# The first down projection of a decoder trunk: the third block product moved ahead of the seventh, its sums made by adding transfers

## The chip, the cores and the metric

The kernel runs on one core of a Trainium2 chip. The metric is the device time of one execution in microseconds (us); it is given as the median of three runs. The engines are named as in the profile: PE (TensorE, matrix products), PEld (its weight loads), DVE (VectorE), ACT (ScalarE), POOL (GpSimd) and SP (SyncE, which here only issues transfers).

## The reference

The computation is one layer of a decoder for 512 tokens of width 1024, all in float32. The changed place is the product with `w_down` in the first of the two SwiGLU blocks.

```python
def swiglu(x, w_gate, w_up, w_down):
    return (jax.nn.silu(x @ w_gate) * (x @ w_up)) @ w_down
...
        x = x + 0.5 * swiglu(rmsnorm(x, ffn1_norm[l]), ffn1_wg[l], ffn1_wu[l], ffn1_wd[l])
        x = x + hybrid_mixer(rmsnorm(x, mix_norm[l]), w_in[l], conv_w[l], conv_b[l], ...)
        x = x + 0.5 * swiglu(rmsnorm(x, ffn2_norm[l]), ffn2_wg[l], ffn2_wu[l], ffn2_wd[l])
    return rmsnorm(x, final_norm)
```

`w_down` has 2816 rows and 1024 columns. The mixer that follows normalises the new rows of x and multiplies them by `w_in`.

## The kernel before

**Products in three parts.** The matrix products keep nearly float32 accuracy on inputs that are rounded to a shorter type (`fp32r`). A weight tile is split into its rounded part `wh` (a copy on ACT) and the remainder `wl` (a subtraction on DVE); the other operand is split in the same way into `ch` and `cl` (`cx` for a narrower pair). PE then multiplies three times: `wh,ch`, `wh,cl` and `wl,ch`. So every tile needs an ACT and a DVE instruction before PE can use it.

**The down projection in quadrants.** `block_down` cuts the operand and the weight into quadrants and forms the product from seven products of sums and differences of quadrants (instead of eight plain ones). Products 1 and 2 take weight blocks as they come from memory (`wr`). Products 5, 6, 3 and 7 take sums of weight blocks. Four of the weight's blocks per row pair are numbered `blocks(0, n)` to `blocks(3, n)`, n = 0 to 4. The operands are differences of quadrants of the hidden rows, held in tiles named `ha`, `hb` and `cr`. The hidden rows are 2816 = 22 x 128; twenty of these groups go into the ten steps of each product (`pairs` = 10, two quadrants), and a "joined" step per product, written `(p, x)`, takes the remaining ones with weight sums `sj`.

**Steps.** The stage is a list, `steps`, of 78 entries. Before the change the order of products is 1, 2, 5, 6, 7, 3, 4:

- steps 0 and 1: the joined steps of products 1 and 2; 2 to 11: product 1; 12 to 21: product 2
- 22 to 31: product 5; 32 and 33: joined steps of 5 and 6; 34 to 43: product 6
- 44 to 53: product 7; 54 and 55: joined steps of 7 and 3; 56 to 65: product 3
- 66: joined step of 4, 67 empty, 68 to 77: product 4

Each step is six matmuls of 128x512: two row groups `m`, three products each (`products1`). Two steps share one *unit*, a 128x1024 pair `wh`, `wl`.

**What sets the order.** The loop at the end of the quoted code walks over the steps, and the order of the code is the order of each engine's queue (`tc.manual_schedule`). Before step i's turn everything else is placed by a step index: `task(i, ...)` puts work into a table, and `tasks_at(i)` emits it behind the products of step i. The unit of a pair is at its step less 4; its operand at its step less `before`; weight fetches further ahead. `then1(i, ...)` does the same for work outside `block_down`: row loads, squares, turned quadrants, and the first fetches of the mixer. SP is the usual queue for transfers (`Q`), POOL the one (`G`) for adding transfers, which add what they read from memory to a tile.

**PSUM.** Each product accumulates in two banks (one for each row group). `CHAIN` lets products 6, 7 and 4 go on in the bank pair of product 1, and product 3 in that of product 5; product 2 has a pair named `aux`. When a product ends, `results1` issues two DVE instructions `xr<-mm,xr` that add the bank's sums, with factor plus or minus 0.5, to a quadrant of the rows `xr`. The next product in the same banks can't go on until DVE has read them.

```python
    ADDS = {1: [(0, 0, -1)], 5: [(1, 1, 1)], 6: [(1, 0, -1)], 3: [(1, 0, -1)], 7: [(1, 1, 1)], 2: [(0, 0, 1)], 4: [(0, 1, 1)]}
    CHAIN = {6: 1, 7: 1, 4: 1, 3: 5}
```

Around `turn_`, before the last step of product 6 (step 43), the loop interleaves the two row groups of steps 42 and 43 and of 44 and 45, so that the first group's sums are complete a while before product 7 wants their bank.

**The weight sums before.** For products 5 and 6 a tile `sm` per row pair is loaded by SP (`blocks(2, n)`), and POOL adds `blocks(3, n)` and later `blocks(0, n)`. For product 7, SP loads the fourths into half tiles `a` (`blocks(3, n)`, ten half loads `a<-w1d`), and DVE subtracts them from `sm` into a new tile `s` (`less`, two instructions `s<-sm,a` of 128x512 per pair). Then POOL adds `blocks(1, n)` to `sm` for product 3. Product 4 splits its weights straight from the fourths, `a`. The operand of product 7, `ch`/`cl` from `cr`, is split six steps ahead.

The names in the profile that have line L250 are issued by the planner's wrapper (`emit`), and transfers have line L238 (`dma_start`).

Of the kernel before, what the change touches and what calls it, by code (L numbers as in the profile page):

```python
# [9 lines left out]
F32 = mybir.dt.float32  # L10
F32R = mybir.dt.float32r
AF = mybir.ActivationFunctionType
ALU = mybir.AluOpType

P = 128
# [240 lines left out]
def hybrid_kernel(ctx, tc, xt, xrow, vec, w1s, w1u, w1d, wm, wki, wrg, watt, wrnn, wout, w2u, w2d, gf, out):  # L256
# [26 lines left out]
    def nm(s):  # L283
        cnt[0] += 1
        return f"{s}_{cnt[0]}"

    def slot(dt=F32, name="s", last=False):
        if loans and last:
            return loans.pop()
        if mixing:  # L290
            plan.free("slot", SLOTS - 2 * COUPLES)
            held = plan.live["slot"]
            spare = [h for h in mixing if plan.key(h) not in held]
            if spare and dt is F32:
                return plan.take("slot", spare[-last])
        return plan.take("whole", plan.take("slot", big.tile([P, S], dt, tag="slot", name=nm(name))))
# [766 lines left out]
    def block_down(wd, plain, pairs, sums, made=None):  # L1063
# [9 lines left out]
        if made:  # L1073
            steps += run_(3, 6) + run_(7) + [(7, x_), (3, x_)] + run_(3, 6, None)
        else:
            steps += run_(7) + [(7, x_), (3, x_)] + run_(3)
        steps += [(4, x_), None] + run_(4)
        index = {s: i for i, s in enumerate(steps)}
        tasks = {}
# [4 lines left out]
        def blocks(b, n):  # L1084
            return wd[b * (pairs // 2) + n]

        units, turned, ra, raws, s7, fourths = {}, {}, {}, {}, {}, {}

        def fetch(key, i):
            def load():  # L1090
                raws[key] = raw.tile([P, WMAX], F32, tag="raw", name=nm("wr"))
                if type(i) is not int:
                    Q.dma_start(raws[key][:, :i.shape[-1]], i)
                    return
                Q.dma_start(raws[key], wd[i])

            return [("SP", 0.6, load, False)]

# [92 lines left out]
        for i in range(0, len(steps), 2):  # L1191
            st = steps[i]
            p, j = st
            if j == pairs:
                if not made:
                    srcs = [lambda k=k: parts_[k] for k in {1: (0, 1), 5: ("w5", 0), 7: (2, 1), 4: (3,)}[p]]
                    task(i - 4, unit(i, *srcs, n=S))
                    continue
                if p in (5, 7):
                    task(i - 4, unit(i, lambda n=(5, 7).index(p): joined[n]))  # L1200
                    continue
                key, src = ("joined", p), {1: wd[2 * pairs], 4: wd[2 * pairs + 1][:, S:]}[p]
                used.append([i - 4, key, src])
                task(i - 4, unit(i, lambda key=key, c=src.shape[-1]: raws[key][:, :c], n=src.shape[-1]))
                continue
            n = j // 2
            assert steps[i + 1] == (p, j + 1) and j % 2 == 0
            if p in (1, 2) or p == 4 and made:
                key = (p, n)
                used.append([i - 4, key, {1: 0, 2: 1, 4: 3}[p] * (pairs // 2) + n])  # L1210
                srcs = [lambda key=key: raws[key]]
            elif made:
                key = (p, n)
                used.append([i - 4, key, made[p][n]])
                srcs = [lambda key=key: raws[key]]
            elif p == 7:
                srcs = [lambda n=n: s7[n]]
            elif p == 4:
                srcs = [lambda n=n, k=k: fourths[n][k] for k in range(2)]
            else:  # L1220
                srcs = [lambda n=n: sums[n]]
            if p == 1:
                task(j, lambda n=n: difference(n))
            if p == 2:
                task(i, lambda n=n: reduced(n))
            if p == 5 and not made:
                def base(n=n):
                    sums.append(couple(F32, "sm"))
                    Q.dma_start(sums[n], blocks(2, n))

                def add(n=n):
                    G.dma_start(sums[n], blocks(3, n), accum_op=ALU.add)

                at = SUMS_AT[n]
                task(at, [("SP", 0.6, base, False)])
                task(at + 3, [("POOL", 1.2, add, False)])
            if p == 7 and not made:
                def held(n=n):
                    fourths[n] = [slot(F32, "a4") for _ in range(2)]
                    for k, t in enumerate(fourths[n]):  # L1240
                        Q.dma_start(t, blocks(3, n)[:, k * S:(k + 1) * S])

                def less(n=n):
                    s7[n] = raw.tile([P, WMAX], F32, tag="raw", name=nm("s7"))
                    for k, t in enumerate(fourths[n]):
                        c = slice(k * S, (k + 1) * S)
                        V.tensor_sub(s7[n][:, c], sums[n][:, c], t)

                task(i - 13, held)
                task(i - 6, less)  # L1250
            if p == 6 and not made:
                def second(n=n):
                    G.dma_start(sums[n], blocks(0, n), accum_op=ALU.add)

                task(index[5, j] - 3, second)
            if p == 3 and not made:
                def fourth(n=n):
                    G.dma_start(sums[n], blocks(1, n), accum_op=ALU.add)

                task(index[7, j] - 4, fourth)  # L1260
            before = {1: 6, 6: 6, 7: i - index[5, j] - 1 if made else 6, 4: i - (index[7, j] if made else index[3, j] + 6)}.get(p, 5)
            if p == 6:
                task(i - before - 1, lambda n=n: V.tensor_sub(a(n, lo), b(n, hi), a(n, hi)))
            if p == 4:
                task(i - before - 1, lambda n=n: V.tensor_sub(a(n, lo), b(n, lo), a(n, lo)))
            task(i - before, operand(p, n))
            task(i - 4, unit(i, *srcs))
# [288 lines left out]
    def keep(s_, half, i):  # L1556
        keep_part(parts1[s_, half], half, i, (lo, hi)[s_])

    for i, (s_, half) in zip((3, 8, 12, firsts1[3]), ((0, 0), (1, 1), (1, 0), (0, 1))):
        then1(i, load_rows, s_, half)  # L1560
    for p, s_, half, at in ((2, 0, 0, 4), (7, 1, 1, 3), (3, 1, 0, 3)):
        then1(lasts1[p] + at, turn_part, s_, half)
        for m in range(2):
            then1(lasts1[p] + at + m, square_row, 2 * s_ + m, half)
            then1(lasts1[p] + at + (5 if p == 3 else 1 + m), keep, s_, half, m)
    for k in range(NQ):
        then1(lasts1[7] + 6 + k, lambda k=k: half_row(k, lo, x[k][:, lo]))
        then1(lasts1[3] + 1 + k, lambda k=k: half_row(NQ + k, hi, x[NQ + k][:, hi]))
        then1(lasts1[3] + 4 + k, lambda k=k: half_row(k, hi, turned_part(parts1[1, 0], k)))
    then1(index[3, 0], lambda: A.activation(small.tile([P, 4], F32, tag="st", name=nm("root"))[:, :1], epst, AF.Sqrt))  # L1570
    for n in range(RAWS):
        then1(index[3, 3 + 2 * n], mixer_fetch)
    then1(index[3, 8], key_fetch)
    then1(index[4, 3], key_begin)
    then1(last - 1, mixer_begin)
    with tc.manual_schedule(engines=ENGINES):
        assert min(d1.tasks) >= 0
        plan.clear()
        cs = decay()
        turn_ = lasts1[6]  # L1580
        for i in range(last):
            if i in (turn_ - 1, turn_ + 1):
                for m in range(2):
                    for k in range(2):
                        products1(i + k, (m,))
            elif i not in (turn_, turn_ + 2):
                products1(i)
            if i and i - 1 != turn_:
                results1(i - 1)
            if i == turn_:  # L1590
                results1(i)
            d1.tasks_at(i)
            if i > index[6, 0]:
                next(cs, None)
            for f_, args in late1.pop(i, ()):
                f_(*args)
        results1(last - 1)
        assert not late1
        for m in range(2):
            for i in range(last, len(steps)):  # L1600
                products1(i, (m,))
            if m:
                mixer_begin()
            result1(4, m, *ADDS[4][0])
            square_row(m, 1)
            if not m:
                mixer_prepare()
        sd, rs1 = (small.tile([P, NQ], F32, tag=t, name=nm("rs")) for t in ("st", "m8"))
        V.tensor_add(sd, ssr[:, :NQ], ssr[:, NQ:])
        A.activation(sd, sd, AF.Sqrt, scale=1.0 / D, bias=epst)  # L1610
        V.reciprocal(rs1, sd)
        mixer_prepare()
# [972 lines left out]
```

## Time and profile before

| | |
|---|---|
| median of 3 runs | 1044.96 us (1044.94 to 1046.19) |
| profiled execution: time of its own | 1045.18 us |
| its span in the profile | 1043.4 us, so 1.78 us lie around the span |
| mean granted TensorE clock | 0.996 |
| PE busy | 1028.1 us, 99% of the span |
| DVE, ACT, POOL busy | 905.6, 712.5 and 195.0 us |
| DMA | 202.81 MB, mean 194 GB/s |
| the stage: first matmul of step 2, last matmul of the stage | 229.11 us, 343.61 us |

The span is a single execution from its first to its last recorded event. A row of a timeline gives the start, the duration, the engine, the line, the operation, the tiles (out <- in) and the shapes; in brackets stands the idle time ahead of the instruction and what ended it. DVE, ACT and PE overlap consecutive instructions a little, so the distance between starts is shorter than the duration shown. The waits of an engine are listed with their sum, their number and the longest.

### The profile page before, as it was taken

The numbers are of one execution on the slowest core, as the hardware profiler recorded it, in microseconds if no ns is written. First come the engines' busy times: TensorE is split into PE (matmuls) and PEld (weight loads), VectorE is DVE, ScalarE is ACT, GpSimd is POOL, SyncE is SP. The second block draws the span as 40 slices with busy tenths as digits, with TensorE's granted clock in tenths as the row PEclk, the third lists the DMA queues.
The fourth block names the chain that finished last, engine by engine and source line by source line (L and its number), as shares of the span: only waits on it lengthen the run. The fifth ranks groups of instructions, "written<-read, shape, count | busy, mean of one in ns | idle before, by whom it ended". The sixth has DMA issues, their size and how long they took to land.

```text
span 1043.4 us, 15243 instructions
## 1 busy us (share of the span) xinstructions
PE 1028.1 (99%) x5250; PEld 875.8 (84%) x5250; DVE 905.6 (87%) x1543; ACT 712.5 (68%) x1198; POOL 195.0 (19%) x243
## 2 busy tenths in 40 slices
PE   9999999999979999999999999999999999999997
PEld 8898888898758778888888888888998888898886
DVE  7988999987889888999998976777889999889886
ACT  8856766656548659878879664467667666658864
POOL 1613333213110020101001110012422333210000
PEclk9999999999989999999999999999999999999999
DMA  9969999899870363424349997893979999986454
GB/s 356 205 166 221 214 232 227 200 264 245 208 163 17 109 180 103 132 88 126 122 141 248 258 239 212 237 337 54 202 212 229 219 232 220 201 219 220 167 186 162
DMA packets 91181, 202.81 MB, mean 194 GB/s; under 512 B 18400, under 2 KB 25696, under 8 KB 91104
## 3 DMA queue, kind: packets, MB, share of 16 engines
q1 hardware_dynamic: 60608, 142.27, 40.1%
q0 software_dynamic: 30208, 59.26, 33.2%
q8 instruction: 41, 0.67, 0.3%
q10 hardware_dynamic: 288, 0.31, 0.1%
q14 instruction: 36, 0.29, 0.1%
HBM read 181.88 MB, written 25.17 MB: 198 GB/s over the span
## 4 chain that ended last, share of the span: by engine, by line
PE 93%; DVE 3%; DMA 1%; issue 1%; ACT 1%; POOL 0%; DVEq 0%; ACTq 0%; POOLq 0%
PE mm L250 70%; PE aux L250 23%; DVE wl L250 1%; DMA ha<-cr 1%; DMA wr<-w1d 1%; PE aux L1333 0%; ACT wh L250 0%; DVE xr L250 0%; DVE cl L250 0%; DVE s L250 0%; POOL ha L238 0%; DVE cr L250 0%; DVE o L250 0%; DVE kw L250 0%; DVE KI L250 0%
## 5 line engine op out<-in xcount | busy, mean ns | idle before, releaser
L250 DVE TENSOR_TENSOR wl<-wr,wh 128x1024 fp32r<-128x1024 f32 (+3 forms) x149 | 177.1, 1189 | 29.2 <-ACT wh L250 28.7
L250 ACT ACTIVATE wh<-wr 128x1024 fp32r<-128x1024 f32 (+2 forms) x148 | 153.1, 1035 | 37.6 <-PE mm L250 18.8
L250 PE MATMUL mm<-cm,wh 128*128 128x512 f32 (+1 forms) x736 | 167.0, 354 | 0.0
L250 PEld LDWEIGHTS mm<-cm,wh 128*128 128x128 f32 x736 | 126.3, 190 | 15.8
L250 PE MATMUL mm<-yn,wh 128*128 128x512 f32 x420 | 130.7, 392 | 0.0
L250 PE MATMUL aux<-cm,wh 128*128 128x512 f32 (+1 forms) x472 | 119.5, 383 | 0.0
L250 PE MATMUL mm<-cm,wl 128*128 128x256 f32 x608 | 108.3, 282 | 0.0
L250 PE MATMUL mm<-wh,ch 128*128 128x512 f32 (+1 forms) x240 | 94.0, 392 | 7.2 <-DVE xr L250 7.2
L250 PEld LDWEIGHTS aux<-cm,wh 128*128 128x128 f32 x472 | 86.0, 188 | 15.6
L250 PEld LDWEIGHTS mm<-cm,wl 128*128 128x128 f32 x608 | 92.2, 190 | 4.7
L250 PE MATMUL mm<-wl,ch 128*128 128x512 f32 (+1 forms) x240 | 94.0, 392 | 0.1
L250 PE MATMUL mm<-wh,cl 128*128 128x512 f32 (+1 forms) x240 | 93.5, 389 | 0.0
L250 PEld LDWEIGHTS mm<-yn,wh 128*128 128x128 f32 x420 | 77.2, 188 | 14.6
L250 PE MATMUL mm<-yn,wl 128*128 128x512 f32 x210 | 81.9, 390 | 0.0
L250 ACT ACTIVATE wh<-a 128x1024 fp32r<-128x1024 f32 (+1 forms) x78 | 62.8, 814 | 19.7 <-DVE a L250 17.2
L250 DVE TENSOR_TENSOR wl<-a,wh 128x1024 fp32r<-128x1024 f32 (+1 forms) x78 | 71.2, 918 | 5.7 <-ACT wh L250 5.0
L250 PE MATMUL aux<-cm,wl 128*128 128x256 f32 x456 | 70.5, 282 | 0.0
L250 PEld LDWEIGHTS aux<-cm,wl 128*128 128x128 f32 x456 | 63.1, 191 | 1.9
L250 PE MATMUL mm<-yh,wh 128*128 128x512 f32 x160 | 62.7, 394 | 0.0
L250 PE MATMUL mm<-yh,wl 128*128 128x512 f32 x160 | 62.1, 390 | 0.0
L250 PE MATMUL mm<-yl,wh 128*128 128x512 f32 x160 | 62.1, 390 | 0.0
L250 PEld LDWEIGHTS mm<-wh,ch 128*128 128x128 f32 x240 | 45.5, 189 | 16.6 <-ACT wh L250 7.6
(392 smaller groups left out, 2320.0 us busy)
## 6 DMA issues: line engine op xcount, KB each, us to landing
wr<-wm SPq DMA_DIRECT2D x39, 512.0 KB, 3.5
w<-w2d SPq DMA_DIRECT2D x20, 512.0 KB, 7.7
wr<-w SPq DMA_DIRECT2D x20, 512.0 KB, 3.5
wr<-w1u SPq DMA_DIRECT2D x19, 512.0 KB, 6.3
s<-w2u SPq DMA_DIRECT2D x36, 256.0 KB, 4.7
wr<-w2u SPq DMA_DIRECT2D x18, 512.0 KB, 6.1
s<-w2u POOLq DMA_DIRECT2D x36, 256.0 KB, 6.6
s<-w1u SPq DMA_DIRECT2D x32, 256.0 KB, 5.3
```

What stands on the lines that cost most here:

```text
L250: return call(*args, **kw)
```

## The change

The change touches `block_down` (in the form that the first down projection uses, `made` is None) and the loop that runs it.

- The order of products becomes 1, 2, 5, 6, 3, 7, 4. Steps 44 to 53 are now product 3, 54 and 55 the joined steps of 3 and 7, and 56 to 65 product 7.
- The tile `sm` gets `blocks(1, n)` for product 3 by POOL directly behind its use in product 6; no DVE instruction reads it in between.
- Product 7's weights come from new half tiles `s` (slots "s3"): SP loads halves of `blocks(2, n)`, and POOL adds halves of `blocks(0, n)`, two steps behind. That is ten half loads and ten half adding transfers; the ten DVE subtractions and the ten half loads of fourths are gone.
- Product 4's weights are fetched as whole blocks `wr`, five fetches of 512 KB. The first two go out on POOL's queue, the others on SP's.
- The operand of product 7 is split in the fifth product (steps 23 to 31) and no longer six steps ahead of its use.
- Four loads of the rows `xr` go out sooner (steps 2, 6, 9 and the start of product 7).
- The interleaving of row groups is now around the last step of product 7 (step 65), where product 4 goes on in the same banks. The turned quadrants change accordingly: another quadrant is turned after product 3 and another after product 7, and four of the eight half-width `yl`/`yh` pairs are made at full width instead.
- The mixer's first fetches move from product 3 to product 4, four steps ahead of their old places in it.

```diff
-            steps += run_(7) + [(7, x_), (3, x_)] + run_(3)
+            steps += run_(3) + [(3, x_), (7, x_)] + run_(7)
...
-                Q.dma_start(raws[key], wd[i])
+                late = not made and key in ((4, 0), (4, 1))
+                (G if late else Q).dma_start(raws[key], wd[i])
...
-                    srcs = [lambda k=k: parts_[k] for k in {1: (0, 1), 5: ("w5", 0), 7: (2, 1), 4: (3,)}[p]]
+                    srcs = [lambda k=k: parts_[k] for k in {1: (0, 1), 5: ("w5", 0), 3: (1, 2), 4: (3,)}[p]]
...
-            if p in (1, 2) or p == 4 and made:
+            if p in (1, 4, 2):
...
             elif p == 7:
-                srcs = [lambda n=n: s7[n]]
-            elif p == 4:
-                srcs = [lambda n=n, k=k: fourths[n][k] for k in range(2)]
+                srcs = [lambda n=n, k=k: s3[n][k] for k in range(2)]
...
             if p == 7 and not made:
-                def held(n=n):
-                    fourths[n] = [slot(F32, "a4") for _ in range(2)]
-                    for k, t in enumerate(fourths[n]):
-                        Q.dma_start(t, blocks(3, n)[:, k * S:(k + 1) * S])
-
-                def less(n=n):
-                    s7[n] = raw.tile([P, WMAX], F32, tag="raw", name=nm("s7"))
-                    for k, t in enumerate(fourths[n]):
-                        c = slice(k * S, (k + 1) * S)
-                        V.tensor_sub(s7[n][:, c], sums[n][:, c], t)
-
-                task(i - 13, held)
-                task(i - 6, less)
+                def base(n=n, k=0):
+                    s3.setdefault(n, []).append(slot(F32, "s3"))
+                    Q.dma_start(s3[n][k], blocks(2, n)[:, k * S:(k + 1) * S])
+
+                def add(n=n, k=0):
+                    G.dma_start(s3[n][k], blocks(0, n)[:, k * S:(k + 1) * S], accum_op=ALU.add)
+
+                for k in range(2):
+                    task(i + k - 14, lambda base=base, k=k: base(k=k))
+                    task(i + k - 12, lambda add=add, k=k: add(k=k))
...
-                task(index[7, j] - 4, fourth)
-            before = {1: 6, 6: 6, 7: i - index[5, j] - 1 if made else 6, 4: i - (index[7, j] if made else index[3, j] + 6)}.get(p, 5)
+                task(index[6, j] - 3, fourth)
+            before = {1: 6, 6: 6, 7: i - index[5, j] - 1, 4: i - (index[7, j] if made else index[3, j] + 6)}.get(p, 5)
...
-    for i, (s_, half) in zip((3, 8, 12, firsts1[3]), ((0, 0), (1, 1), (1, 0), (0, 1))):
+    for i, (s_, half) in zip((2, 6, 9, firsts1[7]), ((0, 0), (1, 1), (1, 0), (0, 1))):
         then1(i, load_rows, s_, half)
-    for p, s_, half, at in ((2, 0, 0, 4), (7, 1, 1, 3), (3, 1, 0, 3)):
+    for p, s_, half, at in ((2, 0, 0, 4), (3, 1, 0, 4), (7, 1, 1, 3)):
         then1(lasts1[p] + at, turn_part, s_, half)
...
     for n in range(RAWS):
-        then1(index[3, 3 + 2 * n], mixer_fetch)
-    then1(index[3, 8], key_fetch)
+        then1(index[4, 3 + 2 * n] - 4, mixer_fetch)
+    then1(index[7, 8], key_fetch)
...
-        turn_ = lasts1[6]
+        turn_ = lasts1[7]
         for i in range(last):
             if i in (turn_ - 1, turn_ + 1):
                 for m in range(2):
-                    for k in range(2):
+                    for k in (0, 1) if i < turn_ else (0, 2):
                         products1(i + k, (m,))
-            elif i not in (turn_, turn_ + 2):
+            elif i not in (turn_, turn_ + 3):
                 products1(i)
```

DVE's queue at the end of the sixth product before the change. `wl` is a weight remainder, `s` the seventh product's sums, `cl` its operand remainder, `cc` small work of another stage, `xr<-mm` the sixth product's row update:

```order
L250 TENSOR_TENSOR wl_3137<-s_530_3111,wh_3136 128x1024
L250 TENSOR_TENSOR s_537_3140<-sm_2408,a_513_3039 128x512
L250 TENSOR_TENSOR s_537_3140<-sm_2408,a_514_3040 128x512
L250 TENSOR_TENSOR cl_3144<-cr_2643,ch_3143 128x512
L250 SCALAR_TENSOR_TENSOR cc<-cc,zt_3068 128x8 x2
L250 TENSOR_TENSOR wl_3169<-s_537_3140,wh_3168 128x1024
L250 TENSOR_TENSOR s_542_3172<-sm_2481,a_519_3064 128x512
L250 TENSOR_TENSOR s_542_3172<-sm_2481,a_520_3065 128x512
L250 TENSOR_TENSOR cl_3176<-cr_2672,ch_3175 128x512
L250 SCALAR_TENSOR_TENSOR cc<-cc,zt_3068 128x8
L250 SCALAR_TENSOR_TENSOR xr_2664<-mm_2608,xr_2664 128x512
L250 SCALAR_TENSOR_TENSOR xr_2664<-mm_2612,xr_2664 128x512
```

Each step of the seventh product brings two subtractions, a weight remainder and an operand remainder here. The same place after the change, where the work ahead of the row update belongs to the third product:

```order
L250 TENSOR_TENSOR wl_3139<-sm_2399,wh_3138 128x1024
L250 SCALAR_TENSOR_TENSOR cc<-cc,zt_3079 128x8
L250 SCALAR_TENSOR_TENSOR cl_3150<-hb_106,ch_3149 128x512
L250 SCALAR_TENSOR_TENSOR cc<-cc,zt_3079 128x8
L250 TENSOR_TENSOR wl_3161<-sm_2408,wh_3160 128x1024
L250 SCALAR_TENSOR_TENSOR cc<-cc,zt_3079 128x8
L250 SCALAR_TENSOR_TENSOR cl_3174<-hb_108,ch_3173 128x512
L250 SCALAR_TENSOR_TENSOR cc<-cc,zt_3079 128x8
L250 SCALAR_TENSOR_TENSOR xr_2654<-mm_2608,xr_2654 128x512
L250 SCALAR_TENSOR_TENSOR xr_2654<-mm_2612,xr_2654 128x512
```

The subtractions `s<-sm,a` are gone, and the operand remainders are those of the third product.

DVE's queue in the fifth product after the change; the rows `cl<-cr` are the seventh product's operand remainders, which did not stand there before:

```order
L250 TENSOR_TENSOR cl_2909<-ha_109,ch_2908 128x512
L250 TENSOR_TENSOR cl_2914<-cr_2616,ch_2913 128x512
L250 TENSOR_TENSOR wl_2924<-sm_2516,wh_2923 128x1024
L250 TENSOR_TENSOR cl_2934<-ha_111,ch_2933 128x512
L250 TENSOR_TENSOR cl_2939<-cr_2643,ch_2938 128x512
L250 TENSOR_TENSOR wl_2961<-sm_2572,wh_2960 128x1024
L250 TENSOR_TENSOR ha_103<-hb_104,ha_103 128x2x256
L250 TENSOR_TENSOR cl_2976<-cr_2672,ch_2975 128x512
```

Before the change the rows between the `wl` and the `cl<-ha` there were the same without the `cl<-cr`.

DVE's queue after the change at the end of the seventh product. `wl_3434` belongs to the unit of step 66, `wl_3458` to that of step 68, and the row update stands behind both:

```order
L250 TENSOR_TENSOR wl_3413<-s_563_3277,wh_3412 128x512
L250 TENSOR_TENSOR wl_3413<-s_566_3290,wh_3412 128x512
L250 TENSOR_TENSOR wl_3434<-sj_2688,wh_3433 128x512
L250 TENSOR_TENSOR wl_3458<-wr_3401,wh_3457 128x1024
L250 SCALAR_TENSOR_TENSOR xr_2654<-mm_2608,xr_2654 128x512
L250 SCALAR_TENSOR_TENSOR xr_2654<-mm_2612,xr_2654 128x512
L250 TENSOR_TENSOR wl_3480<-wr_3425,wh_3479 128x1024
```

Before the change no product went on in the banks of `mm_2608` and `mm_2612` at this place: the third, in the fifth's banks, ended here.

POOL's queue after the change, at the end of the ten adding half transfers (`s`) of the seventh product's sums; `ha` and `hb` from `wrg` belong to the mixer:

```order
L238 DMA s_559_3252<-w1d 128x512
L238 DMA s_560_3261<-w1d 128x512
L250 MEMSET ha_103 128x128
L238 DMA s_563_3277<-w1d 128x512
L250 AFFINE_SELECT ha_103<-ha_103 128x128
L238 DMA ha_103<-wrg 128x256
L238 DMA s_566_3290<-w1d 128x512
L238 DMA wr_3401<-w1d 128x1024
L238 DMA wr_3425<-w1d 128x1024
L238 DMA hb_104<-wrg 128x256 x2
```

Before the change the rows of `ha_103` and `hb_104` followed one another, directly behind the last adding transfer to a whole tile `sm`; the transfers of `s` and `wr` are new in this queue.

More of the change, by code (lines that the diff above doesn't have):

```diff
@@ L1085, in blocks @@
             return wd[b * (pairs // 2) + n]
-        units, turned, ra, raws, s7, fourths = {}, {}, {}, {}, {}, {}
+        units, turned, ra, raws, s3 = {}, {}, {}, {}, {}
         def fetch(key, i):
@@ L1564, in hybrid_kernel @@
             then1(lasts1[p] + at + m, square_row, 2 * s_ + m, half)
-            then1(lasts1[p] + at + (5 if p == 3 else 1 + m), keep, s_, half, m)
+            then1(lasts1[p] + at + (5 if p == 7 else 1 + m), keep, s_, half, m)
     for k in range(NQ):
-        then1(lasts1[7] + 6 + k, lambda k=k: half_row(k, lo, x[k][:, lo]))
-        then1(lasts1[3] + 1 + k, lambda k=k: half_row(NQ + k, hi, x[NQ + k][:, hi]))
-        then1(lasts1[3] + 4 + k, lambda k=k: half_row(k, hi, turned_part(parts1[1, 0], k)))
+        then1(lasts1[7] + 1 + k, lambda k=k: y.append(norm_tile(k, V_GM, False)))
+        then1(lasts1[7] + 5 + k, lambda k=k: half_row(NQ + k, hi, turned_part(parts1[1, 1], k)))
     then1(index[3, 0], lambda: A.activation(small.tile([P, 4], F32, tag="st", name=nm("root"))[:, :1], epst, AF.Sqrt))
     for n in range(RAWS):
-        then1(index[3, 3 + 2 * n], mixer_fetch)
-    then1(index[3, 8], key_fetch)
+        then1(index[4, 3 + 2 * n] - 4, mixer_fetch)
+    then1(index[7, 8], key_fetch)
     then1(index[4, 3], key_begin)
```

## Prediction

> **What bounds the kernel.** I read the page first, for the engine that is the bound and for the slices where it is not.
>
> ```profile
> span 1043.4 us, 15243 instructions
> PE 1028.1 (99%) x5250; PEld 875.8 (84%) x5250; DVE 905.6 (87%) x1543; ACT 712.5 (68%) x1198; POOL 195.0 (19%) x243
> ...
> PE   9999999999979999999999999999999999999997
> ```
>
> PE is busy 99% of the span, so only what keeps PE from working, or its clock, can cost time. Slice 12 (from 287 us) shows a 7. The waits of PE, sorted, name it:
>
> ```profile
> PE mm L250 <- DVE xr L250: 7.2, 1, 7.2
> PE aux L250 <- DVE kw L250: 1.1, 1, 1.1
> ```
>
> One wait carries nearly everything that PE loses: it wants a PSUM bank that DVE's row update `xr<-mm,xr` hasn't yet read. In PE's timeline:
>
> ```profile
> 229.11 0.39 PE L250 MATMUL mm<-wh,ch 128*128 128x512 f32 x1
> ...
> 256.31 0.39 PE L250 MATMUL mm<-wh,ch 128*128 128x512 f32 x1
> ...
> 288.04 0.40 PE L250 MATMUL mm<-wl,ch 128*128 128x512 f32 x1
> 295.66 0.77 PE L250 MATMUL mm<-wh,ch 128*128 128x512 f32 x1 [7.22 <-DVE xr L250]
> ...
> 298.36 0.47 PE L250 MATMUL mm<-wh,ch 128*128 128x512 f32 x1
> ...
> 313.45 0.39 PE L250 MATMUL mm<-wh,ch 128*128 128x512 f32 x1
> ```
>
> From 229.11 to 256.31 lie steps 2 to 21, 120 matmuls: 27.20 / 120 = 0.2267 us each, 1.36 us a step. The sixth product's last matmul starts at 288.04; the seventh's first is due at 288.27 and starts at 295.66. The next six starts take 2.70 us, about 0.43 each, so PE also runs slowly for a while. Step 56, 72 matmuls after 288.27, starts at 313.45. DVE in the gap, grouped (busy us, mean ns, idle before) and by time:
>
> ```profile
> L250 DVE TENSOR_TENSOR s<-sm,a 128x512 f32<-128x512 f32 x6 | 3.9, 684 | 0.0
> L250 DVE TENSOR_TENSOR wl<-s,wh 128x1024 fp32r<-128x1024 f32 x3 | 3.7, 1222 | 0.6 <-ACT wh L250 0.6
> ```
> ```profile
> 289.31 1.28 DVE L250 TENSOR_TENSOR s<-sm,a 128x512 f32<-128x512 f32 x2
> 290.52 0.69 DVE L250 TENSOR_TENSOR cl<-cr,ch 128x512 fp32r<-128x512 f32 x1
> 291.12 0.36 DVE L250 SCALAR_TENSOR_TENSOR cc<-cc,zt 128x8 f32<-128x8 f32 x2
> 291.81 1.23 DVE L250 TENSOR_TENSOR wl<-s,wh 128x1024 fp32r<-128x1024 f32 x1 [0.32 <-ACT wh L250]
> 292.95 1.29 DVE L250 TENSOR_TENSOR s<-sm,a 128x512 f32<-128x512 f32 x2
> ...
> 294.83 1.28 DVE L250 SCALAR_TENSOR_TENSOR xr<-mm,xr 128x512 f32<-128x512 f32 x2
> ```
>
> DVE is busy, not waiting: the subtractions that make the seventh product's sums, its weight remainders and its operand remainders all stand ahead of the row update. In its queue one half costs 0.60 us (290.52 to 291.12) and a full `wl` 1.14 (291.81 to 292.95). PE resumes 295.66 - 294.83 = 0.83 us after the update starts.
>
> **A. The stall goes.** After the change the third product follows the sixth. It accumulates in the fifth's banks, which DVE read long before, so no step waits for the sixth's row update. Its sums come from adding transfers. Step 56 would start at 288.27 + 72 x 0.2267 = 304.59, against 313.45: **-8.86 us** (7.39 the gap, 1.47 the slow matmuls after it). The rows showed six slow starts in 2.70 us. [...]
>
> **B. Five operand splits move earlier.** The `ch`/`cl` of the seventh product's five operands now go out at steps 23 to 31, in the fifth product: 5 x 0.60 = 3.0 us more of DVE there. What stands there now:
>
> ```profile
> 262.00:283.50 21.50, 21.38 (x97) 17.16 (x96) 18.72 (x26) 14.50 (x24) 2.61 (x3) 1.00 0.94 243
> ```
> ```profile
> DVE wl L250 <- ACT wh L250: 2.1, 3, 0.9
> DVE cl L250 <- ACT ch L250: 0.7, 1, 0.7
> ```
> ```profile
> PEld mm L250 <- DVE wl L250: 1.3, 4, 0.5
> ```
> ```profile
> 265.70 0.63 ACT L250 ACTIVATE ch<-ha 128x512 fp32r<-128x512 f32 x1 [5.19 <-DMA ha<-cr]
> ```
>
> The first is a window of the fifth and sixth products (length; then busy time of PE, PEld, DVE, ACT, POOL; clock; DMA share; GB/s): DVE has 18.72 of 21.50 us. The second: its 2.8 us of idle time are four waits for ACT. The third: PE already waits 1.3 us in four places for DVE's `wl`, so DVE paces PE here and leads by a microsecond at most. The last shows why ACT is late: an operand transferred by POOL landed at 265.70. Bounds: nothing, if the 2.8 us of waits take up nearly all of the 3.0; +3.0, if none. Laying the new order out by hand with these durations, I get +0.6 if that operand lands by 263 (the ten half loads `a<-w1d` that ran beside it are gone, but ten others take their place somewhat later), and +2.1 if it lands as now. I take the middle, **+1.3**.
>
> **C. A new neighbourhood in one bank.** The seventh product is now directly ahead of the fourth, in the same bank pair. The code interleaves the row groups there, so that the first group's sums are done two half steps, 1.36 us, before its bank is wanted. But DVE's row update now stands behind the `wl` of the unit of step 68, whose `wh` buffer comes free with step 63. From the end T of step 63: `wh` about 1.0 us, `wl` 1.14 and the pass from ACT to DVE, so DVE is free at about T + 2.4 and PE goes on 0.83 later, T + 3.2; it is due at T + 2 x 1.36 = T + 2.7. **+0.5**; nothing if ACT gets its buffer a step earlier, and up to 2.7 if DVE comes later by the two steps' length.
>
> **D. Row loads ahead of weight loads.** On SP the 512 KB row load that followed a weight load now precedes it.
>
> ```profile
> 238.54 1.06 ACT L250 ACTIVATE wh<-wr 128x1024 fp32r<-128x1024 f32 x1 [0.37 <-DMA wr<-w1d]
> ```
> ```profile
> xr<-xrow SPq DMA_DIRECT2D x1, 512.0 KB, 6.7
> ```
>
> ACT was waiting for that weight at 238.5; the row load, issued at about 233.9, landed at 240.6. Swapped, the weight lands there, 2.1 to 2.3 us later. Rounding (1.06) and remainder (1.14) then end at about 242.9, and by the pace of 1.36 us PE wants it at about 243.2. So **+0.2**; bounds 0 and 2.3.
>
> **E. What goes and comes beside PE.** Ten `s<-sm,a` (6.0 us of DVE) vanish; six of them were part of A. Eight `yl` halves become four whole ones, late, where DVE has room: 0. On the queues: POOL gets ten adding half transfers and two weight fetches; SP swaps ten half loads of fourths for ten of thirds and gets three weight fetches, and the mixer's first fetches come later.
>
> ```profile
> 303.00:328.00 25.00, 25.00 (x116) 20.77 (x115) 19.53 (x28) 18.14 (x31) 2.98 (x5) 1.00 0.33 85
> 328.00:342.00 14.00, 14.00 (x67) 11.69 (x66) 13.40 (x27) 11.87 (x28) 0.00 (x0) 1.00 0.03 9
> ```
> ```profile
> sm<-w1d POOLq DMA_DIRECT2D x5, 512.0 KB, 5.6
> ```
>
> DMA is idle by two thirds from 303 us and almost wholly from 328, and POOL's transfers from 287 us on land 5.6 us after issue. The last adding transfer, issued at about 304.5, lands by 311 and its sum is wanted at about 313; the fourth product's first weight lands at about 312 and is wanted at 318. The mixer's fetches of 326 to 332 lie 5 us ahead of the stage's end (about 337). Cover: that idle DMA time. Price 0; without it, the fourth rival.
>
> **Sum:** -8.86 + 1.3 + 0.5 + 0.2 = -6.86. The profiled execution took 1045.18 (span 1043.4 and 1.78 around it): 1038.3. It stands 0.22 above the median of the runs, 1044.96, so I say 1038.2. A measurement of this kernel can tell about 0.2%, 2.1 us, from no change: faster is below 1042.9, slower above 1047.1.
>
> **Rivals.**
> 1. The work is only moved: B at its full 3.0, with C at 1.0. For it: PE's four waits for `wl`, which show DVE without a lead. Against: DVE's 2.8 idle us. -8.86 + 3.0 + 1.0 + 0.2 = -4.7: 1040.3.
> 2. No new wait: B, C and D all at nothing or near it. For it: the idle 2.8 us nearly equal the added 3.0, and ten competing half loads leave the stretch. -8.86: 1036.1.
> 3. The second product's weights are late, D at 2.3. For it, ACT's wait at 238.54; against it, the 0.3 us of room that the working leaves. -4.8: 1040.2.
> 4. Slower: POOL's single queue can't deliver the seventh product's sums and the fourth's first weight. In a crowded stretch its transfers landed one behind another:
>
> ```profile
> 257.13 0.89 POOL L238 DMA_DIRECT2D sm<-w1d  x1 [1.02 <-DVE wl L250]
> ...
> 269.44 0.89 POOL L238 DMA_DIRECT2D sm<-w1d  x1 [2.56 <-DVE wl L250]
> ```
> ```profile
> sm<-w1d POOLq DMA_DIRECT2D x1, 512.0 KB, 5.5
> ```
> ```profile
> sm<-w1d POOLq DMA_DIRECT2D x1, 512.0 KB, 10.1
> ```
>
> The one issued at 257.13 took 5.5 us (262.6), the one at 269.44, five transfers later, 10.1 (279.5): 16.9 / 5 = 3.4 us apart. From 289 us at t each, the eleventh, the fourth product's first weight, lands at 289 + 11t and is needed by 318.1; PE then loses 11t - 29.1, and about 1.4 of slow matmuls. At t = 3.4 that is 9.7, the sum +2.3 with C left out: 1047.3. It cancels the gain at t = 3.2 and is slower by over 0.2% from t = 3.4. Between 3.0 and 3.4 there is no change that can be told. Against it: the new transfers are half as large, DMA is idle two thirds of the time, and the later ones land in 5.6. [...]
>
> **Chances.** The forecast (1036.9 to 1039.6) 0.50; rival 1 0.20; rival 2 0.15; rival 3 0.04; rival 4 with t between 3.0 and 3.4, no change, 0.06; above, slower, 0.05. Faster 0.89, no change 0.06, slower 0.05. The range goes from rival 2's end with a little more saved on clock, 1035.6, to rival 1 with B full and C at 2.7, 1042.0; it leaves out rival 4 alone.
>
> **What would show it.** A: no wait of PE for `xr` near 288 and full clock there; step 56 near 304.6 plus what B and D cost. B: more PE waits for `wl` or `cl` between 262 and 283. C: a wait of PE for `xr` of about 0.5 us near 321. D: a wait near 243. E: no PE wait that goes back to `s<-w1d` or `wr<-w1d` from 304 on, stage end near 337. I am wrong if the 7 us come back at 321 behind DVE, or if the sums' transfers land 3 us apart.

## The result and the profile after

The changed kernel takes 1036.93 us (median of four runs, 1036.43 to 1037.22). The ratio to the kernel before is 0.9916, with a 95% interval from 0.9899 to 0.9933: faster by 0.8%, some 8.7 us against the median of 1045.58 that the kernel before has with a fourth run. The forecast was 1038.2, in a range from 1035.6 to 1042.0. The profiled execution took 1037.22, its span is 1035.4, so 1.8 us lie around it. The page of the changed kernel:

```profile
span 1035.4 us, 15245 instructions
PE 1026.7 (99%) x5250; PEld 874.6 (84%) x5250; DVE 899.0 (87%) x1529; ACT 712.1 (69%) x1194; POOL 204.3 (20%) x255
...
PE   9999999999999999999999999999999999999997
```

The 7 of slice 12 is gone. The waits of PE, in order of size:

```profile
PE aux L250 <- DVE kw L250: 1.1, 1, 1.1
...
PE mm L250 <- DVE wl L250: 0.3, 1, 0.3
PE mm L250 <- DVE xr L250: 0.2, 1, 0.2
```

The wait of 7.2 us for the row update at the turn from the sixth product is gone; the 0.2 us that are left for a row update stand at step 66. PE's timeline, at steps 2, 22, 44, 56 and 66 and at the mixer's first product:

```profile
229.59 0.39 PE L250 MATMUL mm<-wh,ch 128*128 128x512 f32 x1
...
256.79 0.39 PE L250 MATMUL mm<-wh,ch 128*128 128x512 f32 x1
...
288.64 0.39 PE L250 MATMUL mm<-wh,ch 128*128 128x512 f32 x1
...
304.96 0.39 PE L250 MATMUL mm<-wh,ch 128*128 128x512 f32 x1
...
319.79 0.70 PE L250 MATMUL mm<-wh,cx 128*128 128x512 f32 x2 [0.16 <-DVE xr L250]
...
336.14 0.48 PE L250 MATMUL mm<-yh,wh 128*128 128x512 f32 x1
```

Two rows of the kernel before that the prediction didn't need, its step 66 and the mixer's first product:

```profile
327.96 0.62 PE L250 MATMUL mm<-wh,cx 128*128 128x512 f32 x2
...
344.20 0.48 PE L250 MATMUL mm<-yh,wh 128*128 128x512 f32 x1
```

Distances between these starts tell where the time came from. "Due" is where step 44 of the kernel before would have begun (288.27).

| stretch | before | after | difference | forecast |
|---|---|---|---|---|
| steps 2 to 22 (D) | 27.20 | 27.20 | 0 | +0.2 |
| step 22 to step 44 due (B) | 31.96 | 31.85 | -0.11 | +1.3 |
| step 44 due to step 56 (A) | 25.18 | 16.32 | -8.86 | -8.86 |
| step 56 to 66 (C) | 14.51 | 14.83 | +0.32 | +0.5 |
| step 66 to the mixer (E) | 16.24 | 16.35 | +0.11 | 0 |
| sum | | | -8.54 | -6.86 |

The spans differ by 8.0: in this execution the work ahead of the changed code ended 0.48 us later (step 2 at 229.59 against 229.11). In the profiles of the other variants, whose code is the same up to there, step 2 began between 229.35 and 230.23.

### The profile page after: what moved, and what is told of

Same layout as the page of the kernel before. It is cut to its first block, busy times and chain, and to the rows that moved or that the text cites. A ratio compares the mean times of both kernels' runs of the same rounds, so it can differ in the third digit from the quotient of the medians.

```text
span 1035.4 us, 15245 instructions
## 1 busy us (share of the span) xinstructions
PE 1026.7 (99%) x5250; PEld 874.6 (84%) x5250; DVE 899.0 (87%) x1529; ACT 712.1 (69%) x1194; POOL 204.3 (20%) x255
## 4 chain that ended last, share of the span: by engine, by line
PE 93%; DVE 4%; DMA 1%; issue 1%; ACT 1%; DVEq 0%; ACTq 0%; POOLq 0%
PE mm L250 69%; PE aux L250 23%; DVE wl L250 1%; DMA ha<-cr 1%; DVE cl L250 1%; DMA wr<-w1d 1%; ACT wh L250 0%; DVE xr L250 0%; PE aux L1329 0%; DVE ha L250 0%; DVE sj L250 0%; DVE cr L250 0%; DVE o L250 0%; DVE kw L250 0%; DVE KI L250 0%
## 5 line engine op out<-in xcount | busy, mean ns | idle before, releaser
L250 DVE TENSOR_TENSOR wl<-wr,wh 128x1024 fp32r<-128x1024 f32 (+3 forms) x154 | 183.2, 1190 | 33.1 <-ACT wh L250 32.6
L250 ACT ACTIVATE wh<-wr 128x1024 fp32r<-128x1024 f32 (+2 forms) x153 | 158.4, 1036 | 42.1 <-PE mm L250 18.0
L250 ACT ACTIVATE wh<-a 128x1024 fp32r<-128x1024 f32 (+1 forms) x68 | 57.1, 842 | 18.2 <-DVE a L250 17.2
L250 DVE TENSOR_TENSOR wl<-a,wh 128x1024 fp32r<-128x1024 f32 (+1 forms) x68 | 64.8, 953 | 5.5 <-ACT wh L250 5.0
L250 ACT ACTIVATE tu<-mm 128x512 f32<-128x512 f32 (+1 forms) x57 | 28.3, 497 | 43.8 <-PE mm L250 43.8
```

What stands on the lines that cost most here:

```text
L250: return call(*args, **kw)
```

## The experiments

The times of the changed kernel and of its variants lie close together, so small differences are read in the profile from step to step. Each ratio is against runs of the kernel before on the same chip.

**1. The sums alone.** The old order, with the new way to make the seventh product's sums (and, not in the excerpt, the fourth's weights fetched whole; the mixer's first fetches move with them).

```diff
-                srcs = [lambda n=n: s7[n]]
+                srcs = [lambda n=n, k=k: s3[n][k] for k in range(2)]
...
-                task(i - 13, held)
-                task(i - 6, less)
+                for k in range(2):
+                    task(i + k - 14, lambda base=base, k=k: base(k=k))
+                    task(i + k - 12, lambda add=add, k=k: add(k=k))
```

> The old order of products (7 ahead of 3), but the seventh product's sums made by the adding half transfers and the fourth's weights fetched whole, as in the changed kernel. Theory (the sums and the order each remove part of the stall): without the two subtractions per pair DVE reaches the row update at about 291 instead of 294.8, the wait of PE at the turn falls from 7.2 to about 3.5 us, and the time is about 1041 us (1040 to 1042.5). Rival 1 (the order alone removes the stall, the subtractions are beside the point): wait still over 6 us, 1044 or more. Rival 2 (the subtractions alone were the stall): wait under 1 us, about 1037.

Measured: 1042.53 us, ratio 0.9968 (0.9955 to 0.9981). PE and DVE at the turn:

```profile
290.36 0.39 PE L250 MATMUL mm<-wl,ch 128*128 128x512 f32 x1
293.79 0.77 PE L250 MATMUL mm<-wh,ch 128*128 128x512 f32 x1 [3.04 <-DVE xr L250]
```
```profile
288.95 1.29 DVE L250 TENSOR_TENSOR wl<-s,wh 128x512 fp32r<-128x512 f32 x2
...
291.07 1.29 DVE L250 TENSOR_TENSOR wl<-s,wh 128x512 fp32r<-128x512 f32 x2
...
292.96 1.28 DVE L250 SCALAR_TENSOR_TENSOR xr<-mm,xr 128x512 f32<-128x512 f32 x2
```

A pair now costs DVE 2.12 us (288.95 to 291.07); before it was 3.64 (288.17 to 291.81). The wait falls from 7.2 to 3.0 us, as expected, but doesn't go: the rest of DVE's queue still stands ahead of the row update. The fifth product became slower at the same time (its last transferred operand came 10.99 us after step 22, before it was 9.39; from step 22 to step 44 due are 33.53 us, before 31.96), which puts the time at the upper edge of what was expected. Both rivals fall: the sums alone take more than half of the stall, and not all of it.

**2. The order alone.** The new order, with ten DVE subtractions, now in place.

```diff
+                def less(n=n):
+                    for k, t in enumerate(s3[n]):
+                        V.tensor_sub(t, sums[n][:, k * S:(k + 1) * S], t)
...
+                task(index[6, j] - 11, held)
+                task(index[6, j] - 4, less)
```

> The changed kernel with its new order, but the seventh product's sums made as before, by ten DVE subtractions of 128x512 (in place, in the sixth product) instead of ten adding transfers. Theory: the turn from the sixth to the next product shows no wait of PE for the row update, but DVE has only about 1.5 us to spare between 262 and 303, so about 4 us of the 6.0 us of subtractions come out as waits of PE for wl or cl: about 1041 us (1039.5 to 1042.5). Rival (the order is all, DVE absorbs the subtractions as it absorbed the operand splits): 1037 us.

Measured: 1041.43 us, ratio 0.996 (0.9944 to 0.9976). Its waits of PE, and its window of the fifth and sixth products (columns as in the prediction):

```profile
PE mm L250 <- DVE wl L250: 3.4, 3, 1.7
```
```profile
262.00:283.50 21.50, 19.82 (x90) 15.80 (x89) 21.30 (x32) 13.78 (x25) 4.34 (x5) 1.00 1.07 266
```

PE has no wait for the row update at this turn, but DVE is busy for 21.30 of 21.50 us and PE waits for `wl`. Steps 22 to 54 take 49.48 us, against 45.45 in the changed kernel and 44.42 in experiment 3: 4 to 5 of the 6.0 us of subtractions come out as time. The rival falls. The order removes the stall, and the subtractions that it leaves on DVE come out elsewhere; the adding transfers make the order worth its full price.

**3. The operand split late again.** It undoes step B.

```diff
-            before = {1: 6, 6: 6, 7: i - index[5, j] - 1, 4: ...
+            before = {1: 6, 6: 6, 7: i - index[5, j] - 1 if made else 6, 4: ...
```

> The changed kernel with the seventh product's operands split six steps ahead of their use again (ch and cl from cr in steps 50 to 58), not in the fifth product. The prediction's step B (the early split costs 1.3 us) expects 1035.6. The reading of the trace after (the early split met no cost, because the last transferred operand landed 2.7 us sooner and DVE's idle time took it up; what is left are 1.4 us of waits for wl in steps 39 to 43) expects between 1036.0 and 1037.0: at most 0.8 us of those waits go, and DVE has room from 299 to 321. A cost on the other side (DVE late for the seventh product's sums) would give 1038 or more.

Measured: 1036.48 us, ratio 0.9912 (0.9898 to 0.9927). Its window of the fifth and sixth products and that of the changed kernel:

```profile
262.00:283.50 21.50, 21.50 (x101) 17.89 (x100) 19.60 (x31) 15.80 (x26) 6.06 (x7) 1.00 1.06 222
```
```profile
262.00:283.50 21.50, 21.16 (x97) 17.09 (x96) 20.57 (x29) 16.23 (x28) 5.21 (x6) 1.00 1.00 192
```

With the late split, steps 22 to 54 take 44.42 us, 1.03 less than in the first profile of the changed kernel. That would fit the prediction's price of B, but the time, 0.45 us less, fits the other reading (1036.0 to 1037.0). Experiments 10 and 11 had to say whether it was the split or the execution.

**4. The early split alone,** in the kernel before (the same line, the other way round).

```diff
-            before = {1: 6, 6: 6, 7: i - index[5, j] - 1 if made else 6, 4: ...
+            before = {1: 6, 6: 6, 7: i - index[5, j] - 1, 4: ...
```

> The kernel before with one part of the change: the seventh product's operands are split in the fifth product. Theory (the early split is free only if the ten half loads of fourths don't hold up the last transferred operand): the wait at the turn falls by the three splits that stood ahead of the row update, 1.8 us, to about 5.4, and the fifth and sixth products become 1 to 2 us longer: 1044 to 1045.5, no change that can be told. Rival (the early split is free wherever it stands): 1043.0.

Measured: 1046.23 us, ratio 0.9998 (0.9987 to 1.0008): no change. But the terms are others than expected. The wait at the turn fell by 0.6 us only (7.22 to 6.66), and the slow matmuls behind it took that back: steps 44 to 54 last 15.72 us, before 15.07. DVE shows why the wait stayed:

```profile
PE mm L250 <- DVE xr L250: 6.7, 1, 6.7
```
```profile
290.45 1.29 DVE L250 TENSOR_TENSOR s<-sm,a 128x512 f32<-128x512 f32 x2
...
292.94 1.23 DVE L250 TENSOR_TENSOR wl<-s,wh 128x1024 fp32r<-128x1024 f32 x1 [0.93 <-ACT wh L250]
294.08 1.29 DVE L250 TENSOR_TENSOR s<-sm,a 128x512 f32<-128x512 f32 x2
```
```profile
291.85 1.06 ACT L250 ACTIVATE wh<-s 128x1024 fp32r<-128x1024 f32 x1 [2.58 <-DVE cc L250]
```

From one pair's subtractions to the next are 3.63 us (290.45 to 294.08), as in the kernel before (289.31 to 292.95, 3.64), although DVE has a split less in it; in its place stands a wait of 0.93 us. A pair is a round trip: DVE subtracts, ACT rounds the new sum, DVE takes the remainder. The splits only filled DVE's time while ACT rounded. So the pace of the pairs ahead of the row update was the length of a chain, not the sum of DVE's work that the prediction read.

**5. Quarter transfers.** Each adding half transfer of the seventh product's sums cut in two.

```diff
+                    for c in (slice(0, S // 2), slice(S // 2, S)):
+                        G.dma_start(s3[n][k][:, c], blocks(0, n)[:, k * S + c.start:k * S + c.stop], accum_op=ALU.add)
```

> The changed kernel with each adding half transfer of the seventh product's sums cut into two quarters: twenty adding transfers of 128 KB instead of ten of 256 KB, the same bytes. It tests the fourth rival of the prediction, POOL's single queue. In the trace after, the halves landed about 2.1 us apart and the sums of steps 60 and 61 were split about 1 us ahead of their use. If the queue's price goes by bytes, nothing changes: 1036.4 to 1037.2. If it goes by transfers, the last sums land some 20 us later and PE waits for them: over 1045. Something between (the issue on POOL's queue, 0.87 us each, ten more) gives 1037 to 1040 with a wait that goes back to s<-w1d between steps 56 and 64.

Measured: 1037.74 us, ratio 0.9917 (0.99 to 0.9934). First the changed kernel's rounding of the halves on ACT, then PE's wait in the experiment, at step 66, and ACT's rounding of the fourth product's first weight ahead of it:

```profile
306.26 0.63 ACT L250 ACTIVATE wh<-s 128x512 fp32r<-128x512 f32 x1 [0.65 <-DMA s<-w1d]
308.78 0.63 ACT L250 ACTIVATE wh<-s 128x512 fp32r<-128x512 f32 x1 [1.31 <-DMA s<-w1d]
310.84 0.63 ACT L250 ACTIVATE wh<-s 128x512 fp32r<-128x512 f32 x1 [1.43 <-DMA s<-w1d]
```
```profile
320.00 0.70 PE L250 MATMUL mm<-wh,cx 128*128 128x512 f32 x2 [0.98 <-ACT wh L250]
```
```profile
316.94 1.06 ACT L250 ACTIVATE wh<-wr 128x1024 fp32r<-128x1024 f32 x1 [0.51 <-DMA wr<-w1d]
```

Twice the transfers cost 1.0 us at step 66 (15.79 us from step 56, against 14.83), not 20: the price goes mostly by bytes. What came late was not a sum but the fourth product's first weight, which stands on POOL's queue behind the twenty adds; the `wl` of step 68 and the row update stand behind it on DVE. The changed kernel's halves did come late, about 2.3 us apart (306.26 to 310.84 is two of them), with ACT waiting for each.

**6 and 9. Without the interleaving.** In 6 the row update also reads the sums after step 66 has added to them, which takes away the wait itself (1037.29 us); it tells nothing of C. In 9 the update is read first, as in the changed kernel.

```diff
-        turn_ = lasts1[7]
+        turn_ = -10
```

> The changed kernel without the interleaving of row groups around the last step of the seventh product. The prediction's step C: the interleaving covers 1.36 us of the row update's time; without it the wait at step 66 grows from 0.16 us to about 1.5, and the time is about 1038.3. Rival (the row update is early enough anyway): 1037.

```diff
-            if i in (turn_ - 1, turn_ + 1):
-                for m in range(2):
-                    for k in (0, 1) if i < turn_ else (0, 2):
-                        products1(i + k, (m,))
-            elif i not in (turn_, turn_ + 3):
-                products1(i)
+            products1(i)
```

> The changed kernel without the interleaving of row groups, the row update still read before the fourth product goes on in its banks. The prediction's step C: without the cover of 1.36 us the wait of PE at step 66 grows from 0.16 us to between 0.8 (the update's own 0.83 us, if DVE is free at once) and 1.5 us: about 1037.6 to 1038.3. Rival (DVE comes late at this place whatever the order, because it stands behind the weight remainder of step 68): 2 us or more, 1039.

Measured: 1037.01 us, ratio 0.9915 (0.9889 to 0.994). PE and DVE of experiment 9 at step 66:

```profile
319.43 0.70 PE L250 MATMUL mm<-wh,cx 128*128 128x512 f32 x2 [0.20 <-DVE xr L250]
```
```profile
317.42 1.23 DVE L250 TENSOR_TENSOR wl<-wr,wh 128x1024 fp32r<-128x1024 f32 x1 [0.79 <-ACT wh L250]
318.59 1.37 DVE L250 SCALAR_TENSOR_TENSOR xr<-mm,xr 128x512 f32<-128x512 f32 x2
```

The wait is 0.20 us, against 0.16. Both theories miss: DVE comes to the row update only when the `wl` of step 68 is done, and by then the first group's sums are complete in either order. The interleaving buys nothing here.

**7 and 8. Row loads back, and two fetches back on SP.**

```diff
-    for i, (s_, half) in zip((2, 6, 9, firsts1[7]), ...
+    for i, (s_, half) in zip((3, 8, 12, firsts1[7]), ...
```

> The changed kernel with the row loads behind the weight loads on SP, where they stood before (steps 3, 8, 12). The prediction's step D priced their move at 0.2 us; the trace after shows no wait from step 2 to step 22. Theory by the trace: no change, 1036.9 within 0.3. Rival: the move cost something that other transfers hid, 0.2 to 1 us faster.

Measured: 1037.62 us, ratio 0.992 (0.99 to 0.994); steps 2 to 22 take 27.20 us as in the first profile of the changed kernel, where D cost nothing. But in experiments 9 and 11, which have the early row loads too, these steps take 27.58 and 27.68 us. In experiment 11 PE waits at step 12 for the remainder of a weight that came late to ACT:

```profile
241.89 1.06 ACT L250 ACTIVATE wh<-wr 128x1024 fp32r<-128x1024 f32 x1 [1.72 <-DMA wr<-w1d]
```
```profile
244.26 0.50 PE L250 MATMUL aux<-wl,ch 128*128 128x512 f32 x1 [0.19 <-DVE wl L250]
```

This is the wait near 243 that the prediction named as D's sign. From issue to landing that weight took 7.5 us here and 6.3 to 7.0 in the other eight profiles with the early row load; in the four with the row load behind it (the kernel before and experiments 1, 4 and 7) it took 4.0 to 5.3. So the later landing is there each time, and PE's room takes it up in seven of nine profiles. Experiment 9 lost its 0.38 us at step 16, behind another late weight. One profile of experiment 7 can't show that late row loads always avoid this.

```diff
-                late = not made and key in ((4, 0), (4, 1))
+                late = False
```

> The changed kernel with the fourth product's first two weight fetches on SP's queue again instead of POOL's. Theory: ACT's rounding of these weights waits for PE to free a buffer, not for the fetch, so nothing changes: 1036.9 within 0.3. Rival: on SP they go out ahead of the half loads' adding transfers and take bandwidth from them, so that the sums of steps 60 and 61 come late: 1037.5 to 1039.

Measured: 1037.88 us, ratio 0.992 (0.9902 to 0.9938). The wait of PE, and ACT's rounding of the last sum in this experiment; then that sum in the changed kernel:

```profile
320.24 0.70 PE L250 MATMUL mm<-wh,cx 128*128 128x512 f32 x2 [1.19 <-DVE xr L250]
```
```profile
313.04 0.62 ACT L250 ACTIVATE wh<-s 128x512 fp32r<-128x512 f32 x1
315.65 0.63 ACT L250 ACTIVATE wh<-s 128x512 fp32r<-128x512 f32 x1 [1.99 <-DMA s<-w1d]
```
```profile
313.60 1.14 ACT L250 ACTIVATE wh<-s 128x512 fp32r<-128x512 f32 x2
```

Its rival holds. On SP the two fetches go out some 10 us sooner (294.55, against 305.32 on POOL) and run beside the adding transfers; the last half sum is late, and step 66 waits 1.19 us. On POOL's queue they go out behind the last add (issued at 304.76).

**10 and 11. The changed kernel and the late split once more,** on one chip; the edits are none and that of experiment 3.

> The changed kernel once more, as the measure for the others on the same chip: 1036.9 within 0.5. In the executions of the other variants whose fifth and sixth products are the same, PE had no wait at steps 39 to 43, where the first profile showed 1.1 us; if those waits vary by execution, this profile may show them or not.

> The changed kernel with the seventh product's operands split late (as in the third experiment), beside the changed kernel on the same chip. If the early split costs something, this is 0.4 to 1.1 us faster than the changed kernel; if the waits at steps 39 to 43 vary by execution and not with the split, the two agree within 0.3.

Measured: 1037.33 us (1036.53 to 1037.96) and 1036.88 us (1036.23 to 1037.15); the times alone don't part them. The profiles do, if each is set beside the time at which ACT could split the last operand that POOL transfers (`ch<-ha`; in 10 and 11):

```profile
262.97 0.63 ACT L250 ACTIVATE ch<-ha 128x512 fp32r<-128x512 f32 x1 [1.80 <-DMA ha<-cr]
```
```profile
263.76 0.63 ACT L250 ACTIVATE ch<-ha 128x512 fp32r<-128x512 f32 x1 [2.46 <-DMA ha<-cr]
```

| execution | split | operand after step 22 | steps 22 to 54 |
|---|---|---|---|
| experiment 8 | early | 5.18 | 44.43 |
| changed kernel, experiment 10 | early | 5.55 | 44.41 |
| experiment 5 | early | 5.66 | 44.44 |
| experiment 9 | early | 6.21 | 44.92 |
| experiment 7 | early | 6.51 | 45.20 |
| changed kernel, first profile | early | 6.72 | 45.45 |
| experiment 3 | late | 5.91 | 44.42 |
| experiment 11 | late | 6.22 | 44.42 |

With the early split every tenth that the operand comes after about 5.7 us is a tenth lost; with the late split 6.22 costs nothing. So the early split costs 0 to 1.0 us by execution, not by its own work but because DVE then has less reserve against a late operand (busy for 20.57 of 21.50 us in the window above, 19.60 with the late split). Experiment 4, early and at 7.24, fits: from step 22 to step 44 due are 32.22 us there, 1.41 more than the 30.81 of the executions without a wait. The operand's own transfer takes 6.28 to 6.34 us in the first profile of the changed kernel and in experiments 3 and 5 to 11; what differs is when POOL issues it, 0.40 us after the start of step 22 in the first profile and 0.75 ahead of it in experiment 10. Why that differs stays open. The late split is the better choice by the steps, by half a microsecond at most in the median, which the times can't confirm.

## Why the prediction was right, and where its terms were off

**A** was right to the hundredth: step 44 due to step 56 takes 16.32 us, 12 steps of 1.36. The little more that the fast end of the range counts as saved on the clock is shown by no run: the stretch runs at a granted clock of 1.00, and what it saves is the gap and the slow matmuls behind it, 8.86 us. Experiments 1 and 2 show that it needs both parts: alone they bring 0.3% and 0.4% of the 0.8%. The reading of why DVE was late was too simple: a round trip with ACT, not DVE's work alone, as experiment 4 shows.

**B** is the term that failed: +1.3, and measured -0.11 in the first profile. In the second (experiment 10), steps 22 and 44 begin here:

```profile
257.42 0.39 PE L250 MATMUL mm<-wh,ch 128*128 128x512 f32 x1
...
288.23 0.39 PE L250 MATMUL mm<-wh,ch 128*128 128x512 f32 x1
```

That is 30.81 us, 1.15 less than before. The failed step is the bound: it ended at nothing, although the prediction had quoted 1.3 us of PE's waits in that stretch as a sign of tightness and not as time that could be won back. They went because operands came sooner, as far as the rows can be followed. In the kernel before, the largest, 0.4 us at step 30, stands behind the `wl` that ACT's `ch<-ha` of 265.70 held up, 9.39 us after step 22; in the changed kernel it came at 6.72. One of 0.2 us at step 22 stands behind an earlier transfer of the same kind; the rest, small waits at steps 40 to 42 among it, is not traced. The layout by hand had +0.6 for an early landing; the early landing also took away what PE lost before. In the first profile the early split then cost 1.0 us at steps 38 to 42, and the two nearly cancel. Of the 2.7 us that the operand came sooner, 1.0 is POOL's issue (1.41 us after step 22 before, 0.40 now); the rest is the transfer itself, and SP's queue shows what no longer runs beside it. Its half loads, before and after:

```profile
253.78 21.10 SPq L238 DMA_DIRECT2D a<-w1d  x10
```
```profile
272.30 22.30 SPq L238 DMA_DIRECT2D s<-w1d  x10
```

They go out 18 us later. The operand's transfer from issue to landing, in the kernel before, in experiment 1 and in experiment 10:

```profile
ha<-cr POOLq DMA_DIRECT2D x1, 256.0 KB, 8.0
```
```profile
ha<-cr POOLq DMA_DIRECT2D x1, 256.0 KB, 9.1
```
```profile
ha<-cr POOLq DMA_DIRECT2D x1, 256.0 KB, 6.3
```

| execution | half loads in flight beside it | issue to landing |
|---|---|---|
| changed kernel, experiments 3 and 5 to 11 | 0 | 6.28 to 6.34 |
| experiment 4 | 1, in its last 1.6 us | 6.41 |
| experiment 2 | 3 | 6.97 |
| kernel before | 4 | 7.95 |
| experiment 1 | 4 | 9.12 |

So the half loads beside it go with a longer transfer; why four of them cost 1.2 us more in experiment 1 than before stays open.

**C** was near: +0.5, measured +0.32, and its working (DVE behind the `wl` of step 68) is what the rows show:

```profile
316.72 1.06 ACT L250 ACTIVATE wh<-wr 128x1024 fp32r<-128x1024 f32 x1 [0.97 <-PE mm L250]
```
```profile
317.81 1.23 DVE L250 TENSOR_TENSOR wl<-wr,wh 128x1024 fp32r<-128x1024 f32 x1 [1.34 <-ACT wh L250]
318.96 1.40 DVE L250 SCALAR_TENSOR_TENSOR xr<-mm,xr 128x512 f32<-128x512 f32 x2
```

Step 63 ends at 316.75, ACT starts there, DVE is free 2.2 us later (2.4 was reckoned), and PE goes on 3.04 us later (3.2). The cover by interleaving, which it counted on, isn't needed: without it the wait is 0.20 us, with it 0.16.

**D** was 0 in this profile instead of 0.2, and 0.4 to 0.5 in two of nine: its mechanism is there, its price varies by execution. **E** was 0.1 instead of 0, but its landings were late: the last half, issued at 304.76, took 9.3 us and not 5.6, and the fourth product's first weight landed at 315.3, where about 312 was reckoned, 1.4 us before ACT took it up.

```profile
s<-w1d POOLq DMA_DIRECT2D x1, 256.0 KB, 9.3
```

The sum was -8.54 instead of -6.86, and most of the difference is B. By these steps the result is nearer to **rival 2** (-8.86), whose absent waits are what B showed, than to the forecast; in experiment 10 the same steps save 9.52. That the time still lies within the forecast's own band, by 0.03 us at its fast end (1036.9), is in part luck: the work ahead of the stage took 0.48 us more than in the profile before, and that offsets some of the larger saving. **Rival 4** was nearer than its chance said: POOL's halves came 2.3 us apart, by the rival's own sum the loss begins at 2.65 (29.1 / 11), and experiments 5 and 8 cost 1.0 us at step 66 by making the queues only a little worse.

## What to carry to other kernels

Where an engine stands between an accumulator's end and its next user, look at what is queued ahead of the read, and reorder so that a product with other banks comes next; then take the work off that queue too, or it comes out as waits elsewhere (in experiment 2, 4 to 5 of 6.0 us). When a stretch loses time now, the lower bound for what a change does there is minus that loss, not zero (here a loss of 1.3 us, and B came out at -0.11 and -1.15). The operand splits that were moved early cost nothing where the last transferred operand came by 5.66 us after step 22 and 1.0 us where it came at 6.72: judge such a move by the slowest landing, over several profiles, since one can miss a wait that shows in two of nine.

## What the runs showed of the hardware

In three profiles the slow matmuls after a stall didn't scale with it. In experiment 1 PE was idle for 3.04 us (its next matmul was due at 290.59 and began at 293.79), and its window around that start reads:

```profile
293.00:297.00 4.00, 3.21 (x8) 2.60 (x9) 3.69 (x12) 1.15 (x2) 0.86 (x1) 0.57 1.10 293
```

The granted clock is 0.57, and its first two steps took 4.16 us instead of 2.72; before, after an idle time of 7.22 us, they took 4.17. So 1.4 us of slow matmuls came with less than half of the stall. Experiment 4, with a wait of 6.66 us, has a clock of 0.50 in the same stretch around its start, nine starts in a row that are 0.42 us apart or more (before: six), and a cost of 2.1 us (15.72 for ten steps instead of 13.60):

```profile
295.40:299.40 4.00, 3.21 (x8) 2.59 (x9) 3.97 (x10) 1.06 (x1) 0.86 (x1) 0.50 0.92 144
```

In these three profiles the slow matmuls thus don't follow the length of the stall. In experiment 2 PE's waits of 1.7 us and less left the clock at 1.00 in the windows from 262 to 303 us.
